# Phase 3 of an encoder layer: the norms listed before the merges, nine 12 KB pieces for its large operands, four buffers for the rows of x

## The chip, the cores and the metric

The kernel runs on one core of one Trainium2 chip. The metric is the device time of one execution in microseconds; before the change the median of 3 runs is 3186.42 us (3184.72 to 3188.18). The engines are named as in the profile: PE (TensorE, matrix products), with PEld for its weight loads, DVE (VectorE), ACT (ScalarE), POOL (GpSimd) and SP (SyncE, which here issues every DMA). PE writes to PSUM; ACT and DVE read PSUM, POOL does not.

## The reference

One layer of an encoder with two request groups, a prompt of 512 tokens and a sample of 1024, with a model width of 1024. All is float32. The part that matters here is the end of the layer:

```python
    merged = g[:, :, 0] * (att @ w_proj_attn) + g[:, :, 1] * (y_ssm @ w_proj_ssm)
    return merged @ w_out
...
        x = x + rmsnorm(m, norm_post_mix[l])
        h = rmsnorm(x, norm_pre_ffn[l])
        gate, up = jnp.split(h @ w_gate_up[l], 2, axis=-1)
        f = (jax.nn.silu(gate) * up) @ w_down[l]
        x = x + rmsnorm(f, norm_post_ffn[l])
```

`g` are sigmoid gates, `att` and `y_ssm` the results of differential attention and of a bidirectional state-space scan. `w_gate_up` is 1024 x 5632, that is gate and up of 2816 columns each.

## The kernel before

The 1536 tokens of both groups are worked on together, in three chunks `c` of 512 (chunk 0 is the prompt). Each float32 operand of a large product is split into two fp32r halves: `hi`, a cast, and `lo`, the rest (`split`, L133: with `act_dve` ACT casts in L135 and DVE subtracts in L136; with `act_pool` ACT casts in L141 and POOL subtracts in L142). A product is three matmuls, hi x hi, hi x lo, lo x hi (`gemm`, L164 to L169).

Phase 3 begins at L872. For each chunk it has three steps:

- the merge: `load_merged(0)` for chunk 0, whose two branches were already merged in phase 2, and `merge(c, ...)` for chunks 1 and 2, which multiplies `w_proj_attn` by the attention's rows and adds the other branch. The result is a pair `hi`, `lo` of 8 x 512 columns (`big_pair`);
- `out_proj`: 16 products of 128 tokens by 256 columns with `w_out`, copied into four tiles `mt`, with sums of squares;
- `norms(c, ...)`: on DVE the first norm (L1066), the added rows of x (loaded in halves into `xr`, L1065, added in L1067), squares on ACT into the same `xr` (L1068), the second norm (L1074); then 32 transposes on PE (L1078), copies `hr` to SBUF (L1080) and stores to `h2` in DRAM (L1081, shown as `h_d`).

Then comes the gate-and-up product, in two halves of 768 tokens. Each half is multiplied by a fast scheme with seven products per block instead of eight: for each of the 22 blocks `jb` of 128 columns of gate and of up, `weights` makes seven weight operands (three of them sums made on POOL, L989, L990, L992, L997), and `gate_up` runs seven products of 12 matmuls and puts them together on DVE. The seven activation operands, `b11`, `t2`, `t3`, `t1`, `b21`, `t4`, `b22` in the order of their products, are made once for each half by `Operands` from rows of `h2` (`rw`, L928): `t2`, `t3`, `t1` and `t4` are sums and differences. The first `NPRE` = 2 blocks run with single buffers in the pool `mp` and make silu from tanh, since `norms(2)` uses the same space; from the third block on a pool `fw` takes the place of `mp`.

All pairs and operands are tiles of one pool, `big`: seven slots of 16 KB a partition. A pair takes two slots, an operand (12 KB) one. A tile waits until an earlier user of its slot is done.

The order of instructions in each engine's queue is set while the program is built, by a planner that simulates the program and lets each engine take, of the instructions that are ready in its simulation, the one listed first. On the chip each queue runs strictly in that order. The places are thus the order of listing in L1087 to L1107 for the norms, merges and operands, and each engine's queue for what then stands behind what. The listing that the change touches:

```python
            t0 = out_proj(m0)
            m1 = merge(1, aT1)
            norms(0, t0)
            aT2 = att(2)
            t1 = out_proj(m1)
            m2 = merge(2, aT2)
            norms(1, t1)
            ops = Operands(0, wk, "araw", 3)
            ops.build_first()
            ops.build(("b21",), V, "act_dve")
            t2 = out_proj(m2)
            ops.build(("t4",), V, "act_dve")
```

Of the kernel before, what the change touches and what calls it, by code (L numbers as in the profile page):

```python
# [10 lines left out]
F32 = mybir.dt.float32  # L11
I32 = mybir.dt.int32
F32R = mybir.dt.float32r
AF = mybir.ActivationFunctionType
ALU = mybir.AluOpType
# [3 lines left out]
P = 128  # L19
D = 1024  # L20
KB = D // P
# [9 lines left out]
SEGK = 120  # L31
SKP = 2304
PU = (1, 1)
OT = ("gt", 2)
NG = 2
YE = ("act_pool",) * 4
RATIO = 0.5
# [1 line left out]
IA = 1  # L39
AHEAD = (0,)  # L40
XRB = 2
NPRE = 2
CB = (1, 1)
RWB = 7
NW = 0
NKEEP = 1
SEQS = ((0, 4), (4, 12))
GROUPS = ((0, 512), (512, 1024))
# [29 lines left out]
def hybrid_trunk_kernel(ctx: ExitStack, tc: tile.TileContext, a: dict, y_prompt, y_sample):  # L78
    nc = tc.nc
    V, S, G, TE = nc.vector, nc.scalar, nc.gpsimd, nc.tensor  # L80
# [3 lines left out]
    def f(ap):  # L84
        return ap.bitcast(F32)
# [273 lines left out]
    with ExitStack() as ph1:  # L359
# [18 lines left out]
        with tc.tile_pool(name="xa", bufs=2, reuse_waits="tile") as xa, tc.tile_pool(name="xa_ps", bufs=3, space=PSUM) as xps:  # L378
            natural_log_exp()
            later = []  # L380
            for c in range(NCH):
                dst = hp.tile([P, 2, KB, 512], F32R, tag="hT", name=f"hT{c}")
                tiles = []
# [134 lines left out]
        for d_ in range(2):  # L518
            for o in (0, 1024):
# [6 lines left out]
                     tag="wraw")  # L526
# [343 lines left out]


    with ExitStack() as ph3:  # L872
        big = ph3.enter_context(tc.tile_pool(name="big", bufs=7, reuse_waits="tile"))
        wk = ph3.enter_context(tc.tile_pool(name="wk", bufs=2, reuse_waits="tile"))
        wy = ph3.enter_context(tc.tile_pool(name="wy", bufs=1, reuse_waits="tile"))
        mm = ph3.enter_context(tc.tile_pool(name="mm", bufs=6, space=PSUM, reuse_waits="tile"))
# [3 lines left out]
        def mm_tile(n):  # L880
            return mm.tile([P, n], F32, tag="mm", name="mm")

        def big_pair():
            return [big.tile([P, KB, 512], F32R, tag="big", name="big") for _ in range(2)]

        def load_merged(c):
            hi, lo = big_pair()
            for k in range(0, KB, 2):
                both = mp.tile([P, 2, 512], F32, tag="mt", name="both", bufs=4)
                load(out=both, in_=part_d[k * P:(k + 2) * P, c * 512:(c + 1) * 512].rearrange("(a p) t -> p a t", p=P))  # L890
                S.activation(out=hi[:, k:k + 2], in_=both, func=AF.Copy, scale=0.5)
                V.scalar_tensor_tensor(lo[:, k:k + 2], both, 0.5, f(hi[:, k:k + 2]), op0=ALU.mult, op1=ALU.subtract)
            return hi, lo

        def merge(c, aTt):
# [21 lines left out]
        class Operands:  # L917
# [4 lines left out]
            def __init__(self, t0, pool, tag, bufs):  # L922
                self.t0, self.pool, self.tag, self.bufs, self.tiles = t0, pool, tag, bufs, {}
# [4 lines left out]
                load(out=x, in_=h2_d[r0:r0 + P, n0:n0 + 384])  # L928
                return x

            def build_first(self):
                b11, t2, t3, t1 = [big.tile([P, 2, 4, 384], F32R, tag="big", name="op") for _ in range(4)]
                self.tiles.update(b11=b11, t2=t2, t3=t3, t1=t1)
                for k in range(4):
                    x, y, z = self.raw(0, 0, k), self.raw(0, 1, k), self.raw(1, 1, k)
                    split(b11[:, 0, k], b11[:, 1, k], x[:], "act_dve")
                    V.tensor_sub(z, z, y)
                    split(t3[:, 0, k], t3[:, 1, k], z[:], "act_dve")
                    V.tensor_sub(y, y, x)
                    split(t1[:, 0, k], t1[:, 1, k], y[:], "act_dve")  # L940
                    V.tensor_add(x, x, z)
                    split(t2[:, 0, k], t2[:, 1, k], x[:], "act_dve")

            def build(self, names, add, eng):
                for name in names:
# [89 lines left out]
        with ExitStack() as ph3a:  # L1035
# [17 lines left out]
            def norms(c, arg):  # L1053
                tiles, sums = arg
                v, r, t_ = [wk.tile([P, 2, 4], F32, tag=n, name=n) for n in ("mv", "mr", "mt_")]
                s2 = wk.tile([P, 4, 2], F32, tag="ms2", name="ms2")
                V.reduce_sum(v[:, 0], sums, axis=mybir.AxisListType.X)
                V.tensor_scalar(v[:, 0], v[:, 0], 1.0 / D, EPS, op0=ALU.mult, op1=ALU.add)
                rsqrt(r[:, 0], v[:, 0], t_[:, 0])
                for j, mt in enumerate(tiles):  # L1060
                    t = 4 * c + j
                    for o in (0, 512):
                        mo = mt[:, o:o + 512]
                        xt = mp.tile([P, 512], F32, tag="xr", name="xr", bufs=2)
                        load(out=xt, in_=rows(t, a["x_prompt"], a["x_sample"])[:, o:o + 512])  # L1065
                        V.scalar_tensor_tensor(mo, mo, r[:, 0, j:j + 1], pmw[:, o:o + 512], op0=ALU.mult, op1=ALU.mult)  # L1066
                        V.tensor_add(mo, mo, xt)  # L1067
                        S.activation(out=xt, in_=mo, func=AF.Square, accum_out=s2[:, j, o // 512:o // 512 + 1])  # L1068
                    store(out=x2_d[t * P:(t + 1) * P, :], in_=mt)
                V.tensor_add(v[:, 1], s2[:, :, 0], s2[:, :, 1])  # L1070
                V.tensor_scalar(v[:, 1], v[:, 1], 1.0 / D, EPS, op0=ALU.mult, op1=ALU.add)
                rsqrt(r[:, 1], v[:, 1], t_[:, 1])
                for j, mt in enumerate(tiles):
                    V.tensor_scalar(mt, mt, r[:, 1, j:j + 1], 0.0, op0=ALU.mult, op1=ALU.add)  # L1074
                for k in range(KB):
                    ps = tr_ps.tile([P, 512], F32, tag="tr", name="tr_ps")
                    for j, xn in enumerate(tiles):
                        TE.transpose(ps[:, j * P:(j + 1) * P], xn[:, k * P:(k + 1) * P], ident)  # L1078
                    hr = (mp if k % 2 else wk).tile([P, 512], F32, tag=("gt", "xr")[k % 2], name="hr", bufs=2)
                    S.activation(out=hr, in_=ps, func=AF.Copy, scale=cols[:, C_FFN + k:C_FFN + k + 1])  # L1080
                    store(out=h2_d[k * P:(k + 1) * P, c * 512:(c + 1) * 512], in_=hr)  # L1081

# [5 lines left out]
            att_scale(1, zq, msq, ap, tr_ps, "tr")  # L1088
            aT1 = att(1)
            t0 = out_proj(m0)  # L1090
            m1 = merge(1, aT1)
            norms(0, t0)
            aT2 = att(2)
            t1 = out_proj(m1)
            m2 = merge(2, aT2)
            norms(1, t1)
            ops = Operands(0, wk, "araw", 3)
            ops.build_first()
            ops.build(("b21",), V, "act_dve")
            t2 = out_proj(m2)  # L1100
            ops.build(("t4",), V, "act_dve")
            ops.tag, ops.bufs = OT
            ops.build(("b22",), V, "act_pool")
            w = {jb: weights(jb, "pt", 1) for jb in range(NPRE + NW)}
            for jb in range(NPRE):
                gate_up(0, jb, ops.all(), w[jb], mp, 1, False)
            norms(2, t2)  # L1107

        with tc.tile_pool(name="fw", bufs=2, reuse_waits="tile") as fw:
            for jb in range(NPRE, FB):  # L1110
                if jb >= NPRE + NW:
                    w[jb] = weights(jb, rpool=fw if jb > NPRE else None)
                gate_up(0, jb, ops.all(), w[jb], fw, 2)
            ops = Operands(768, fw, "rw", RWB)
            ops.build_first()
            ops.build(ops.names[4:], G, "act_dve")
            for jb in reversed(range(FB)):
                if jb < FB - NKEEP:
                    w[jb] = weights(jb, rpool=fw)
                gate_up(768, jb, ops.all(), w[jb], fw, 2)  # L1120
# [104 lines left out]
```

## Time and profile before

| | |
|---|---|
| median of 3 runs | 3186.42 us |
| the profiled execution | 3193.28 us |
| its span, first to last instruction | 3191.5 us |
| PE busy | 3035.2 us (95%) |
| DVE busy | 1826.8 us (57%) |
| ACT busy | 1260.0 us (39%) |
| POOL busy | 650.7 us (20%) |
| mean granted clock of PE | 0.980 |

The profile is of one execution. In its groups a line is followed by the engine, the operation, the output and input tiles by name, the shapes, the count, the busy time and the mean of one in ns, then the idle time of the engine just before and what ended it. `L167 <- ACT whi L135: 18.5, 2, 15.6` in the view of waits reads: instructions of line 167 waited for ACT's line 135 writing `whi`, 18.5 us in all, 2 times, 15.6 us the longest. A timeline gives the start, the duration, the instruction, and in brackets the idle time before it and its releaser. Matmuls are pipelined, so that a matmul's own duration is longer than the distance to the next.

### The profile page before, as it was taken

The page shows a single profiled execution, that of the slowest core. Times are in us where ns is not written, and L with a number is a line of the kernel's source. Part 1 is how long each engine was busy: PE and PEld are TensorE (multiplying, and loading weights), DVE is VectorE, ACT ScalarE, POOL GpSimd, SP SyncE. Part 2 cuts the span into 40 slices and gives each one's busy share as a digit, 9 for nine tenths or more (in the row PEclk, how much of TensorE's full clock was granted, in tenths as well). Part 3 has the DMA queues.
Part 4 walks back from the last instruction along what each step waited for, and adds up shares of the span by engine and source line. Part 5 has one row for each costly group of instructions (what it writes and reads, how often), then busy time and mean ns, then how long its engine had stood idle before and what let it go on. Part 6 is the DMA issues. An engine that isn't in the chain of part 4 may idle for free. (4 is left out here: it accounts for less than half of the span.)

```text
span 3191.5 us, 44134 instructions
## 1 busy us (share of the span) xinstructions
PE 3035.2 (95%) x16667; PEld 2672.3 (84%) x16667; DVE 1826.8 (57%) x2957; ACT 1260.0 (39%) x2305; POOL 650.7 (20%) x508
## 2 busy tenths in 40 slices
PE   7999999999999999899999898978999999989998
PEld 7988887888787777788877787878999899978887
DVE  5214444455327996387778845676666766632444
ACT  4103333333303333366666645543333333332443
POOL 0001111000133442243232100023333433300000
PEclk9999999999999999999999999989999999999999
DMA  4633333223554445755546047644333333363454
GB/s 149 195 99 112 110 105 108 59 77 106 156 166 139 146 143 150 213 174 165 168 135 186 27 139 240 214 145 130 98 103 101 100 98 100 108 202 97 125 163 132
DMA packets 441341, 429.44 MB, mean 135 GB/s; under 512 B 25200, under 2 KB 358481, under 8 KB 440017
## 3 DMA queue, kind: packets, MB, share of 16 engines
q1 hardware_dynamic: 441129, 426.63, 43.2%
q8 instruction: 131, 2.15, 0.3%
q14 instruction: 81, 0.66, 0.1%
HBM read 314.48 MB, written 120.44 MB: 136 GB/s over the span
## 5 line engine op out<-in xcount | busy, mean ns | idle before, releaser
L167 PE MATMUL acc<-hT,whi 128*128 128x512 f32 x1056 | 421.6, 399 | 3.4 <-ACT st L453 3.4
L168 PE MATMUL acc<-hT,whi 128*128 128x512 f32 x1056 | 417.1, 395 | 0.0
L169 PE MATMUL acc<-hT,wlo 128*128 128x512 f32 x672 | 262.5, 391 | 0.0
L167 PEld LDWEIGHTS acc<-hT,whi 128*128 128x128 f32 x1056 | 199.1, 189 | 49.1 <-issue 5.8
L299 ACT ACTIVATE pt<-pt,nm 128x1024 f32<-128x1024 f32 (+1 forms) x192 | 193.1, 1006 | 111.3 <-DVE nm L296 108.0
L168 PEld LDWEIGHTS acc<-hT,whi 128*128 128x128 f32 x1056 | 199.2, 189 | 42.6 <-issue 3.6
L296 DVE CUSTOM_DVE_ANT_0 pt<-s,tb 128x1024 f32<-128x1024 f32 (+1 forms) x192 | 197.5, 1040 | 53.0 <-PE s L294 41.0
L167 PE MATMUL acc<-whi,hT 128*128 128x256 f32 x768 | 224.9, 293 | 1.2 <-ACT hT L206 0.6
L169 PE MATMUL acc<-whi,hT 128*128 128x256 f32 x768 | 225.1, 294 | 0.4 <-DVE hT L207 0.3
L168 PE MATMUL acc<-wlo,hT 128*128 128x256 f32 x768 | 223.3, 291 | 0.0
L167 PE MATMUL d<-dhi,fh 128*128 128x512 f32 x528 | 207.1, 392 | 5.9 <-ACT fh L135 5.9
L169 PE MATMUL d<-dhi,fl 128*128 128x512 f32 x528 | 206.8, 392 | 4.2 <-DVE fl L136 4.2
L168 PE MATMUL d<-dlo,fh 128*128 128x512 f32 x528 | 206.8, 392 | 0.0
L135 ACT CAST whi<-wraw 128x1024 fp32r<-128x1024 f32 (+1 forms) x115 | 115.9, 1036 | 214.0 <-PE acc L169 82.9
L136 DVE TENSOR_TENSOR fl<-raw,fh 128x896 fp32r<-128x896 f32 (+1 forms) x70 | 79.5, 1137 | 193.7 <-ACT fh L135 193.7
L167 PE MATMUL mm<-op,wy 128*128 128x384 f32 x528 | 178.9, 339 | 8.6 <-ACT op L135 6.9
L234 POOL TENSOR_TENSOR ql<-raw,qh 128x512 fp32r<-128x512 f32 x48 | 64.7, 1362 | 575.0 <-ACT qh L231 575.0
L169 PE MATMUL mm<-op,wy 128*128 128x384 f32 x528 | 178.7, 339 | 0.0
L168 PE MATMUL mm<-op,wy 128*128 128x384 f32 x528 | 178.4, 338 | 0.0
L136 DVE TENSOR_TENSOR wlo<-wraw,whi 128x1024 fp32r<-128x1024 f32 x80 | 95.4, 1221 | 112.9 <-ACT whi L135 103.5
L167 PEld LDWEIGHTS acc<-whi,hT 128*128 128x128 f32 x768 | 147.9, 193 | 11.7 <-issue 9.6
L169 PE MATMUL acc<-hT,whi 128*128 128x512 f32 x384 | 156.3, 407 | 0.0
(356 smaller groups left out, 8200.5 us busy)
## 6 DMA issues: line engine op xcount, KB each, us to landing
wraw<-in_w_in_dram SPq DMA_DIRECT2D x60, 512.0 KB
wraw<-in_w_gate_up_dram SPq DMA_DIRECT2D x92, 256.0 KB
raw<-ff_d SPq DMA_DIRECT2D x46, 448.0 KB
wr<-in_w_gate_up_dram SPq DMA_DIRECT2D x80, 256.0 KB
ff_d<-c SPq DMA_DIRECT2D x88, 192.0 KB
g_d<-st SPq DMA_DIRECT2D x48, 256.0 KB
xg<-xs_d SPq DMA_DIRECT2D x48, 256.0 KB
gt<-g_d SPq DMA_DIRECT2D x48, 256.0 KB
```

The costliest lines, as they stand in the source:

```text
L135: S.copy(hi, raw)
L136: V.tensor_sub(lo, raw, f(hi))
L167: TE.matmul(ps, ah, bh, start=(i == 0), stop=False)
L168: TE.matmul(ps, ah, bl, start=False, stop=False)
L169: TE.matmul(ps, al, bh, start=False, stop=(i == n - 1))
L234: G.tensor_sub(q_l[:, s_], q_r[:, s_], f(q_h[:, s_]))
L296: V.tensor_tensor_reduce(out=pt[:], in0=sps[:], in1=tb[:, off:off + SL], scale=-1.0, scalar=3.0e38, op0=ALU.add, op1=ALU.min, accum_out=nm ...
L299: S.activation(out=pt, in_=pt, func=AF.Exp, bias=nm[:, m:m + 1], scale=-1.0, accum_out=(z0, zs[:, 0:1])[m])
```

## The change

The pool `big` has nine slots of 12 KB instead of seven of 16 KB (108 KB instead of 112). A pair is now three slots: each holds three of the eight blocks of 512 columns, both their `hi` and `lo`; a small class `Part` maps the index `k` to the slot. An operand still takes one slot. `load_merged` converts each loaded pair of blocks in two steps of 512 columns instead of one of 1024.

`norms(0)` and `norms(1)` are listed ahead of `merge(1)` and `merge(2)`. The rows `xr` have four buffers instead of two; every second `hr` uses them, and the first half's operands take their rows from them instead of from `araw` (three buffers) and, for `b22`, `gt` (two). `t4` is listed ahead of `out_proj(2)`; the weights of block 0 are listed ahead of `b22`, whose subtraction goes from POOL to DVE; the weights of the other early blocks are listed one block at a time. `NPRE` is 4 instead of 2.

For the second half `build_first`, which loads three rows for each k-block and makes four operands of them, gives way to `build` by terms: `b11` and `t2` with their sums on POOL, `t3` and `t1` with theirs on DVE, each loading its own rows (1, 3, 2 and 2 for each k-block instead of 3 together). Its `b21`, `t4` and `b22` are as before.

```diff
-OT = ("gt", 2)
...
-NPRE = 2
+NPRE = 4
...
-        big = ph3.enter_context(tc.tile_pool(name="big", bufs=7, reuse_waits="tile"))
+        big = ph3.enter_context(tc.tile_pool(name="big", bufs=9, reuse_waits="tile"))
...
+        class Part:
+
+            def __init__(self, tiles, part):
+                self.tiles, self.part = tiles, part
+
+            def __getitem__(self, at_):
+                k = at_[1]
+                return self.tiles[k // 3][(at_[0], self.part, k % 3) + at_[2:]]
+
         def big_pair():
-            return [big.tile([P, KB, 512], F32R, tag="big", name="big") for _ in range(2)]
+            tiles = [big.tile([P, 2, 3, 512], F32R, tag="big", name="big") for _ in range(3)]
+            return Part(tiles, 0), Part(tiles, 1)
...
-                S.activation(out=hi[:, k:k + 2], in_=both, func=AF.Copy, scale=0.5)
-                V.scalar_tensor_tensor(lo[:, k:k + 2], both, 0.5, f(hi[:, k:k + 2]), op0=ALU.mult, op1=ALU.subtract)
+                for i in range(2):
+                    S.activation(out=hi[:, k + i], in_=both[:, i], func=AF.Copy, scale=0.5)
+                    V.scalar_tensor_tensor(lo[:, k + i], both[:, i], 0.5, f(hi[:, k + i]), op0=ALU.mult, op1=ALU.subtract)
...
-                        xt = mp.tile([P, 512], F32, tag="xr", name="xr", bufs=2)
+                        xt = mp.tile([P, 512], F32, tag="xr", name="xr", bufs=4)
...
-                    hr = (mp if k % 2 else wk).tile([P, 512], F32, tag=("gt", "xr")[k % 2], name="hr", bufs=2)
+                    hr = (mp if k % 2 else wk).tile([P, 512], F32, tag=("gt", "xr")[k % 2], name="hr", bufs=(2, 4)[k % 2])
...
             t0 = out_proj(m0)
+            norms(0, t0)
             m1 = merge(1, aT1)
-            norms(0, t0)
             aT2 = att(2)
             t1 = out_proj(m1)
+            norms(1, t1)
             m2 = merge(2, aT2)
-            norms(1, t1)
-            ops = Operands(0, wk, "araw", 3)
+            ops = Operands(0, mp, "xr", 4)
             ops.build_first()
-            ops.build(("b21",), V, "act_dve")
+            ops.build(("b21", "t4"), V, "act_dve")
             t2 = out_proj(m2)
-            ops.build(("t4",), V, "act_dve")
-            ops.tag, ops.bufs = OT
-            ops.build(("b22",), V, "act_pool")
-            w = {jb: weights(jb, "pt", 1) for jb in range(NPRE + NW)}
+            w = {0: weights(0, "pt", 1)}
+            ops.build(("b22",), V, "act_dve")
             for jb in range(NPRE):
+                if jb:
+                    w[jb] = weights(jb, "pt", 1)
                 gate_up(0, jb, ops.all(), w[jb], mp, 1, False)
             norms(2, t2)
...
             ops = Operands(768, fw, "rw", RWB)
-            ops.build_first()
+            ops.build(ops.names[:2], G, "act_dve")
+            ops.build(ops.names[2:4], V, "act_dve")
             ops.build(ops.names[4:], G, "act_dve")
```

More of the change, by code (lines that the diff above doesn't have):

```diff
@@ L41 @@
 XRB = 2
-NPRE = 2
+NPRE = 4
 CB = (1, 1)
 RWB = 7
-NW = 0
 NKEEP = 1
@@ L929, in raw, with build_first @@
                 return x
-            def build_first(self):
-                b11, t2, t3, t1 = [big.tile([P, 2, 4, 384], F32R, tag="big", name="op") for _ in range(4)]
-                self.tiles.update(b11=b11, t2=t2, t3=t3, t1=t1)
+            def build_first(self, names=("b11", "t2", "t3", "t1")):
+                o = {n: big.tile([P, 2, 4, 384], F32R, tag="big", name="op") for n in names}
+                self.tiles.update(o)
                 for k in range(4):
                     x, y, z = self.raw(0, 0, k), self.raw(0, 1, k), self.raw(1, 1, k)
[L936 to L942, printed above, removed]
+                    for n, t_, m, s_ in (("b11", x, None, None), ("t3", z, z, y), ("t1", y, y, x), ("t2", x, x, z)):
+                        if m is not None and (n in o or n != "t1"):
+                            (V.tensor_add if n == "t2" else V.tensor_sub)(t_, m, s_)
+                        if n in o:
+                            split(o[n][:, 0, k], o[n][:, 1, k], t_[:], "act_dve")
             def build(self, names, add, eng):
@@ L1110, in hybrid_trunk_kernel @@
             for jb in range(NPRE, FB):
-                if jb >= NPRE + NW:
-                    w[jb] = weights(jb, rpool=fw if jb > NPRE else None)
+                w[jb] = weights(jb, rpool=fw if jb > NPRE else None)
                 gate_up(0, jb, ops.all(), w[jb], fw, 2)
             ops = Operands(768, fw, "rw", RWB)
-            ops.build_first()
+            ops.build(ops.names[:2], G, "act_dve")
+            ops.build(ops.names[2:4], V, "act_dve")
             ops.build(ops.names[4:], G, "act_dve")
```

## The prediction

> **What bounds the kernel now.** I read the page first, for the engine that is full:
>
> ```profile
> span 3191.5 us, 44134 instructions
> PE 3035.2 (95%) x16667; PEld 2672.3 (84%) x16667; DVE 1826.8 (57%) x2957; ACT 1260.0 (39%) x2305; POOL 650.7 (20%) x508
> ```
>
> PE is the bound, so only time in which PE stands or runs slowly can be won. The change touches phase 3 alone, about 1840 to 2800 us. So I cut that phase into stages in the table of windows (columns: stretch, its length, busy time and instructions of PE, PEld, DVE, ACT, POOL, granted clock, DMA share, GB/s):
>
> ```profile
> 2100.00:2185.00 85.00, 53.19 (x275) 48.33 (x274) 63.04 (x110) 32.94 (x71) 30.59 (x19) 0.82 0.49 156
> 2470.00:2500.00 30.00, 19.42 (x81) 18.56 (x81) 29.85 (x44) 14.06 (x30) 18.73 (x13) 0.77 0.37 110
> 1895.00:1960.00 65.00, 59.88 (x305) 50.64 (x306) 53.55 (x96) 32.69 (x63) 0.00 (x0) 0.97 0.82 277
> 1960.00:1985.00 25.00, 19.65 (x143) 19.02 (x142) 6.31 (x8) 15.49 (x39) 0.00 (x0) 0.86 0.49 162
> 2060.00:2100.00 40.00, 39.10 (x327) 38.80 (x326) 21.46 (x36) 25.91 (x72) 0.00 (x0) 1.00 0.55 183
> 2650.00:2700.00 50.00, 50.00 (x289) 50.00 (x288) 31.27 (x56) 17.05 (x34) 16.67 (x14) 1.00 0.35 106
> ```
>
> The last row is the gate-and-up product undisturbed: 50 / 289 = 0.173 us a matmul, and 84 matmuls (seven products of 12) make 14.5 us for a block `jb`. Against it three places are poor: the entry to the first half of that product (2100 to 2185), the change of halves (2470 to 2500), and the seam after the first merge (1960 to 1985). In the view of waits, PE in 2100 to 2185:
>
> ```profile
> PE mm L167 <- ACT whi L135: 18.5, 2, 15.6
> PE tr_ps L1078 <- DVE mt L1074: 7.7, 1, 7.7
> PE mm L169 <- DVE whi L136: 2.1, 1, 2.1
> PE mm L167 <- ACT c L1021: 1.7, 1, 1.7
> PE tr_ps L1078 <- ACT hr L1080: 0.9, 2, 0.6
> PE mm L169 <- DVE wlo L136: 0.8, 1, 0.8
> ```
>
> Together 31.7 us. After the 15.6 us the clock is low as well; PE's timeline there:
>
> ```profile
> 2117.96 0.69 PE L167 MATMUL mm<-op,whi 128*128 128x384 f32 x1 [15.57 <-ACT whi L135]
> ...
> 2124.73 0.52 PE L168 MATMUL mm<-op,wlo 128*128 128x384 f32 x1
> 2125.05 0.38 PE L167 MATMUL mm<-op,wlo 128*128 128x384 f32 x1
> ```
>
> From 2118 to 2125 a matmul follows the last after 0.32 us; 7 us at about half speed lose some 3.4. So about 35 of the 85 us are lost. Why `whi` is late stands in POOL's timeline:
>
> ```profile
> 2109.42 4.13 POOL L142 TENSOR_TENSOR op<-rw,op 128x384 fp32r<-128x384 f32 x2 [301.13 <-DVE rw L951]
> 2113.51 1.66 POOL L989 TENSOR_TENSOR s<-wraw 128x512 f32<-128x512 f32 x1
> 2115.24 2.01 POOL L990 TENSOR_TENSOR s<-s,wraw 128x512 f32<-128x512 f32 x1
> ```
>
> PE's second product needs `s2` (L990) of the first block's weights. That stands on POOL behind `b22`'s subtractions (L142), which wait for a slot that `out_proj(2)` frees. DVE is just then building `t4`, which waits for a slot too.
>
> **Entry to the first half: -25 us.** Seven slots less `m2`'s two left five for operands until `out_proj(2)` ended: `b11`, `t2`, `t3`, `t1`, `b21`. Nine slots less three leave six, so `t4` (12 adds and 4 splits on DVE) moves under `out_proj(2)`, where DVE is busy 21.46 of 40 us. With `b22` off POOL and listed after `weights(0)`, nothing stands ahead of L989 and L990, which here follow L142 with no wait of their own. So the first wait, the 2.1 behind it and the slow clock go: 15.6 + 2.1 + 3.4 = 21. Next late is `b22`, alone behind `out_proj(2)` now: PE needs it six products later, 6 x 12 x 0.173 = 12.5 us. A row of `h2` takes some 5 us to land (below) and its four pieces are cast and subtracted in some 3 (4 x 0.55 and a cast), so it is in time by 4; if its loads come in two rounds, 1 us late.
>
> The 7.7 us are `norms(2)`: its transposes stood after two blocks, now after four, with 29 us more PE work as cover. That cover is used by DVE. Its prices, from the groups of 1890 to 1965, then of 2100 to 2185:
>
> ```profile
> L1067 DVE TENSOR_TENSOR mt<-mt,xr 128x512 f32<-128x512 f32 x8 | 5.5, 688 | 0.6 <-DMA xr<-in_x_prompt_dram 0.6
> ...
> L1066 DVE SCALAR_TENSOR_TENSOR mt<-mt,mr,pmw 128x512 f32<-128x512 f32 x8 | 5.4, 750 | 0.0
> L1074 DVE TENSOR_SCALAR mt<-mt,mr 128x1024 f32<-128x1024 f32 x4 | 2.8, 749 | 0.0
> L184 DVE TENSOR_TENSOR mt__17030<-mr 128x4 f32<-128x4 f32 x6 | 1.0, 162 | 0.2
> ```
>
> ```profile
> L136 DVE TENSOR_TENSOR wlo<-s,wlo 128x512 fp32r<-128x512 f32 x7 | 5.0, 745 | 2.1 <-ACT wlo L135 2.1
> ...
> L1013 DVE SCALAR_TENSOR_TENSOR c<-th,c 128x384 f32<-128x384 f32 x4 | 2.2, 552 | 0.0
> ```
>
> One `norms`: 5.4 + 5.5 + 2.8 and 26 small steps of 0.16 = 18 us. A block with the tanh form: 11 steps of 0.55 and 7 splits of 0.7 = 11 us; the two blocks more in that form cost 4 steps, 2.2 us of it. Four blocks less the first weights (done under `out_proj(2)`), `norms(2)` and `b22` (2.2): 39 + 18 + 2 = 59 us on DVE, against 4 x 14.5 = 58 of matmuls and 32 transposes on PE. That is even, but for POOL: each block has four POOL steps of about 1.3 us, 21 us for four. What DVE loses beside POOL is seen at the change of halves:
>
> ```profile
> 2487.61 0.54 DVE L1022 TENSOR_TENSOR c<-mm,c 128x384 f32<-128x384 f32 x1
> ...
> 2493.70 7.40 DVE L136 TENSOR_TENSOR op<-rw,op 128x384 fp32r<-128x384 f32 x8
> ```
>
> Eight splits of 0.55 took 7.4, 3.0 more, and POOL is busy 18.73 of those 30 us, so 4.6 of the 7.4: DVE loses 0.65 of POOL's time. A `c` add, which reads PSUM, kept its 0.54. With 7 of 18 steps of that kind I take half of 21, 10 us (bounds 0 and 14). Single `c` buffers and one pair of raw weights, which cost 0.8 + 1.7 now, I take at 2 more. So some 10 of the 35 us stay: **-25**, bounds -35 and -5 (only POOL's queue mended).
>
> The Trainium skill, SBUF — State Buffer, section "Who interferes with whom", has DVE and GpSimd hold their shared ports by an exclusive lock. The trace agrees in part, the splits by 0.65 of POOL's time; by the full lock DVE would lose 21 instead of 10, and this term would be -14.
>
> **Change of halves: -7 us.**
>
> ```profile
> 2473.77 0.69 PE L167 MATMUL mm<-op,whi 128*128 128x384 f32 x1 [3.66 <-ACT op L135]
> 2492.89 1.10 PE L167 MATMUL mm<-op,wy 128*128 128x384 f32 x2 [6.92 <-ACT op L135]
> ```
>
> 81 x 0.173 = 14 of 30 us, so 16 are lost: 10.6 in these waits, the rest by the clock of 0.77. Two spare slots now let `b11` and `t2` be built during the blocks before, where DVE has 19 of 50 us free, so the first wait goes. But PE then comes about 5 us earlier to `t4`, whose adds on POOL begin only after `b21`:
>
> ```profile
> 2480.07 5.66 POOL L951 TENSOR_TENSOR rw<-op 128x384 f32<-128x384 f32 x3 [11.09 <-DVE op L136]
> ```
>
> So the gain is what `t4` gains. DVE had 28 steps ahead of `b21`'s (16 splits, 12 adds), and has 16 (`t3`, `t1`): 12 x 0.55 = 6.6. I take -7, bounds -16 and 0. Building by terms costs 20 loads more:
>
> ```profile
> L928 SPq DMA_DIRECT2D rw<-h_d x40: 319/320/743, 1962.5 to 2495.1; - x40
> ```
>
> 20 x 0.32 = 6.4 us of SP's queue and 3.9 MB, where the DMA share is 0.35: nothing, with PE's blocks as cover; without cover 6.4.
>
> **Norms first: -4 us.** In 1890 to 1985 PE waits
>
> ```profile
> PE mm L169 <- DVE wlo L136: 3.8, 2, 2.2
> PE mm L167 <- ACT msq L1050: 3.8, 1, 3.8
> ```
>
> The second comes from `msq` waiting for a buffer behind stores of `h2` (`hr`), at the end of `norms(0)`, inside `out_proj(1)`. Listed first and with four row buffers, the norms end inside the merge, so it goes; the first, a panel split behind other DVE work, stays. What moves ahead of a merge on SP's queue is 8 loads of x and 12 stores, 20 x 0.32 = 6.4 us of issues; behind them stand the merge's panels, its gates and parts, and the panel in hand (48 matmuls of 512 columns, some 10 us) covers them; without that PE would wait those 6.4. `norms(1)` ends earlier too, so the operands' rows start earlier; they share the four buffers with x and `hr`, so a row can wait for a store on SP with `w_out`'s panels behind it. A round costs a landing, from the chain:
>
> ```profile
> 2073.85 4.85 DMA rw<-h_d
> ```
>
> Four rounds for the first four operands and one for `b21`, 24 us, and the 16 steps of `t4`, 9, fit into the 40 us of `out_proj(2)`. Bounds: -15 (all that seam, with its clock of 0.86) and +45 (third rival).
>
> **Entry of the phase: 0.** `load_merged` works in halves:
>
> ```profile
> L892 DVE SCALAR_TENSOR_TENSOR big<-both,big x4: 1218/1220/1222, 1846.8 to 1850.6; 128x1024 fp32r<-128x1024 f32 x4
> ```
>
> 8 x 0.69 instead of 4 x 1.22 is 0.6 us more, but its first piece is ready 0.5 earlier; bounds -1 and +2. In phase 4, other slots come free in another order; the down weights' casts may shift by 2 us either way.
>
> **Sum**: -25 - 7 - 4 = -36. The profiled execution took 3193.28 us (span 3191.5), 7 over the median of 3186.42; I take the difference from the median: **3150 us**.
>
> **The rivals.** *POOL holds DVE for all of its time* in the four blocks: 21 us instead of 10, 11 less gain, 3161. For it: the eight splits; against it: the adds from PSUM. [...] *DVE stays the bound*: 59 us of work with less than 3 idle, and a planner that fixed each queue's order by its own times; the wait for weights turns into waits for splits and `t4` is no earlier; some 6 us are left, 3181. For it: DVE was busy 63 of 85 us; against it: its half-idle `out_proj(2)`. *Norms starve the merge* (slower): in both merges 18 us of `norms` stand in DVE's queue ahead of a panel's split. With its one panel in hand PE stands from 10 us of unbroken norms on, at most 18 us and 3.4 of slow clock, twice 21.4 = 43. With -4 gone: 3186.4 - 32 + 43 = 3197. For it: 53.55 of 65 us of DVE busy in the first merge; against it: the norms' steps are broken by their loads, and the same work in the same stretch cost PE 3.8 us. *Everything goes*: -35 - 16 - 15 = -66, 3120.
>
> **How the numbers follow.** Forecast 0.54, lock 0.13, DVE bound 0.11, starved merge 0.11, everything 0.11. About 0.2%, 6.4 us, is what a measurement tells from no change. Faster: 0.54 + 0.13 + 0.11 = 0.78; same 0.11; slower 0.11. The range leaves out the starved merge and reaches to the rest: 3120 to 3186.
>
> **What would show it.** Right: in the stage after `out_proj(2)` no wait of PE over 5 us; L990 of the first block before `out_proj(2)` ends; four blocks, then the transposes; at the change of halves one wait of PE, for `t4`, instead of two; the norms' transposes inside the merges. Wrong: waits of PE for `wlo` L136 in the merges over 5 us, or DVE full and PE waiting for `c` and `wy` in the four blocks.

## The result, and the profile after

The changed kernel takes **3205.61 us** (median of 6 runs, 3199.01 to 3214.43) where the kernel before takes 3185.1 (6 runs): ratio **1.0063, 95% interval 1.0047 to 1.0079**. It is slower by 0.6%; the forecast was 3150. The profiled execution took 3214.43 us, 21.15 more than the 3193.28 of the one before. The page after:

```profile
span 3212.7 us, 44180 instructions
PE 3044.9 (95%) x16667; PEld 2674.7 (83%) x16667; DVE 1838.6 (57%) x2965; ACT 1260.5 (39%) x2309; POOL 657.9 (20%) x512
```

The engines carry out nearly the same instructions, PE exactly as many; PE stands still or runs slowly for longer. To see where, I took from both traces the starts of the matmuls and added up, for each stage, by how much the distance to the next one exceeds the distance of that shape in undisturbed stretches (0.173 us for 384 columns). This is PE's lost time, waits and slow clock together. The entry is counted to 4 us past the start of the last transpose of `norms(2)`, here and in all runs below:

```
us lost by PE                                           before  after
seam: end of out_proj(0) to end of out_proj(2)           21.8   51.2
entry: from there to just past the norms(2) transposes   40.0   23.3
behind it, up to 25 us before the change of halves        4.9   17.8
change of halves (65 us)                                 16.6   13.1
sum                                                      83.3  105.4
```

The difference, 22.1 us, accounts for the whole difference of the two executions, 21.15. The seam, 207.0 us long before and 237.2 after, lost 29 us more; the entry gained 17 and lost 13 of them again in the blocks behind it; the change of halves gained 3.5. Line numbers after are those before less 2 for `split` and `gemm` (a matmul waits in L165 to L167), and plus 7 to 9 in the merge and the norms (gate rows L914, their tanh L915, their use L919; the norms' transposes L1085, `hr` L1087, its store L1088).

**The seam.** The view of waits, PE in 1895 to 2100 after (it answers to the lines `wlo` L136 and `msq` L1050 of before):

```profile
PE mm L165 <- DVE gt L919: 21.6, 4, 10.1
PE tr_ps L1085 <- ACT hr L1087: 5.9, 6, 1.6
PE tr_ps L1085 <- DVE mt L1081: 3.8, 1, 3.8
PE mm L165 <- ACT msq L1057: 2.6, 1, 2.6
PE mm L167 <- DVE wlo L134: 1.8, 2, 1.2
```

The first line is new: PE has filled the six PSUM buffers that the kernel gives to such products with those of the merge, and waits for DVE to multiply one by its gate row. The wait for `wlo` is smaller than before. The timeline of the same stretch shows why the gate rows are late:

```profile
1935.82 0.92 SPq L1088 DMA_DIRECT2D h_d<-hr  x2
...
1937.71 3.76 SPq L1088 DMA_DIRECT2D h_d<-hr  x4
...
1944.56 0.41 SPq L1088 DMA_DIRECT2D h_d<-hr  x1
...
1945.49 0.48 SPq L914 DMA_DIRECT2D gt<-g_d  x1
...
1950.27 0.63 ACT L915 ACTIVATE gt<-gt 128x512 f32<-128x512 f32 x1 [6.03 <-DMA gt<-g_d]
1950.93 0.69 DVE L919 SCALAR_TENSOR_TENSOR gt<-gt,mm 128x512 f32<-128x512 f32 x1 [14.48 <-ACT gt L915]
...
1951.68 0.80 PE L165 MATMUL mm<-big,whi 128*128 128x512 f32 x1 [9.10 <-DVE gt L919]
```

The first gate row is loaded behind the eighth store of `norms(0)`'s `hr` (2, 4, 1 at 1943.32, and 1), and in SP's waits of 1895 to 2000 its load waits for such a store to land:

```profile
SPq L914 <- DMA h_d<-hr: 1.8, 1, 1.8
```

DVE stands idle for 14.48 us, then PE goes on 0.75 us after DVE began. In the kernel before the gate rows of both merges came in from 1904.3 us on, after from 1945.5 (columns: shortest, median and longest issue in ns, first and last start):

```profile
L905 SPq DMA_DIRECT2D gt<-g_d x16: 319/336/762, 1904.3 to 2054.0; - x16
```
```profile
L914 SPq DMA_DIRECT2D gt<-g_d x16: 319/320/484, 1945.5 to 2088.3; - x16
```

The clock falls with it (table of windows, after: the third value from the end is the granted clock):

```profile
1930.00:1940.00 10.00, 6.60 (x24) 4.16 (x24) 5.74 (x10) 4.77 (x7) 0.00 (x0) 0.52 0.69 208
1940.00:1950.00 10.00, 1.97 (x8) 1.57 (x8) 0.00 (x0) 2.50 (x4) 0.00 (x0) 0.50 0.96 330
1950.00:1960.00 10.00, 8.32 (x24) 6.59 (x25) 5.47 (x8) 3.73 (x6) 0.00 (x0) 0.61 0.46 134
```

**Entry and behind it.** PE's waits in 2130 to 2265 after; the 15.6 us for `whi` are gone, in their place stand many short ones:

```profile
PE mm L165 <- DVE c L1033: 9.1, 2, 5.8
PE mm L165 <- ACT whi L133: 4.6, 3, 2.9
PE tr_ps L1085 <- DVE c L1020: 2.8, 1, 2.8
```

**Change of halves**, PE in 2455 to 2535 after; before there were 10.6 us for `op`:

```profile
PE mm L165 <- DVE c L1034: 3.2, 1, 3.2
PE mm L166 <- DVE op L134: 3.0, 2, 2.7
PE mm L165 <- DVE c L1033: 1.1, 1, 1.1
```

### The profile page after: what moved, and what is told of

It reads as the page before. It is cut to its first block, busy times and chain, and to the rows that moved or that the text cites. A ratio compares the mean times of both kernels' runs of the same rounds, so it can differ in the third digit from the quotient of the medians.

```text
span 3212.7 us, 44180 instructions
## 1 busy us (share of the span) xinstructions
PE 3044.9 (95%) x16667; PEld 2674.7 (83%) x16667; DVE 1838.6 (57%) x2965; ACT 1260.5 (39%) x2309; POOL 657.9 (20%) x512
## 4 chain that ended last, share of the span: by engine, by line
PE 65%; DMA 12%; DVE 9%; issue 5%; ACT 4%; POOL 3%; SPq 1%; ACTq 0%; DVEq 0%; POOLq 0%
PE acc L165 9%; PE acc L167 9%; PE acc L166 9%; PE mm L165 5%; PE mm L166 4%; PE mm L167 4%; PE d L167 4%; PE d L166 4%; PE d L165 4%; DMA raw<-k_d 1%; DMA araw<-r_d 1%; DMA wraw<-in_w_gate_up_dram 1%; DMA gt<-g_d 1%; PE s L291 1%; PE t L306 1%
## 5 line engine op out<-in xcount | busy, mean ns | idle before, releaser
L165 PE MATMUL acc<-hT,whi 128*128 128x512 f32 x1056 | 421.3, 399 | 3.6 <-ACT st L451 3.6
L167 PE MATMUL acc<-hT,wlo 128*128 128x512 f32 x672 | 262.2, 390 | 0.0
L165 PEld LDWEIGHTS acc<-hT,whi 128*128 128x128 f32 x1056 | 199.1, 189 | 49.8 <-issue 5.8
L165 PE MATMUL acc<-whi,hT 128*128 128x256 f32 x768 | 224.2, 292 | 0.5 <-ACT hT L204 0.4
L167 PE MATMUL acc<-whi,hT 128*128 128x256 f32 x768 | 224.0, 292 | 0.4 <-DVE hT L205 0.3
L165 PE MATMUL d<-dhi,fh 128*128 128x512 f32 x528 | 206.5, 391 | 5.9 <-ACT fh L133 5.9
L167 PE MATMUL d<-dhi,fl 128*128 128x512 f32 x528 | 206.1, 391 | 4.2 <-DVE fl L134 4.2
L165 PE MATMUL mm<-op,wy 128*128 128x384 f32 x528 | 179.5, 340 | 1.5 <-ACT c L1028 1.1
L167 PE MATMUL mm<-op,wy 128*128 128x384 f32 x528 | 179.5, 340 | 0.0
L167 PE MATMUL acc<-hT,whi 128*128 128x512 f32 x384 | 156.3, 407 | 0.0
L165 PEld LDWEIGHTS acc<-whi,hT 128*128 128x128 f32 x768 | 147.5, 192 | 10.5 <-issue 9.2
L133 ACT CAST fh<-raw 128x896 fp32r<-128x896 f32 (+1 forms) x70 | 68.8, 984 | 218.2 <-PE d L166 190.2
```

The source lines that it names most:

```text
L133: S.copy(hi, raw)
L165: TE.matmul(ps, ah, bh, start=(i == 0), stop=False)
L167: TE.matmul(ps, al, bh, start=False, stop=(i == n - 1))
```

## The experiments

**Why are the gate rows late?** Theory A: the rows `gt` of a merge, every second `hr` of the norms and `msq` are tiles of one tag with two buffers, and the tiles of a tag take its buffers in the order of listing. With the norms listed first, the merge's gate rows wait until the norms are over and their `hr` stored. The prediction's own rival was DVE's queue. The first run takes the sharing away, the second the order, the third brings the order alone into the kernel before.

```diff
-                    hr = (mp if k % 2 else wk).tile([P, 512], F32, tag=("gt", "xr")[k % 2], name="hr", bufs=(2, 4)[k % 2])
+                    hr = mp.tile([P, 512], F32, tag="xr", name="hr", bufs=4)
```

> The changed kernel, with all eight rows hr of a norm in the four xr buffers, so that the norms no longer use the two gt buffers that the merge's gate rows use. From the end of the first output projection to the end of the third the changed kernel took 237 us, the kernel before 207. Theory A (shared gt buffers: the tiles of a tag take its buffers in the order of listing, so the merge's gate rows wait until the norms' hr are stored): that stretch falls to 205 to 212 us, the gate rows of the first merge are loaded before 1920 us and no PE wait in a merge is over 3 us; the time is 3175 to 3183. Theory B (18 us of norms stand in DVE's queue ahead of the merge's work): the stretch stays within 5 us of 237 and the time at 3200 to 3210, since DVE's order of listing is untouched. Theory C (the norms' loads and stores stand ahead of the gate rows on SP's queue): most of it stays, 225 to 237 us, time over 3193.

Measured: 3169.82 us, ratio to the kernel before 0.9955 [0.9937, 0.9973]; seam 197.9 us, further down than theory A's 205 to 212, lost 13.1. The gate rows and PE's waits in 1885 to 2090 of that run:

```profile
L914 SPq DMA_DIRECT2D gt<-g_d x16: 319/339/1297, 1895.0 to 2040.8; - x16
```
```profile
PE mm L167 <- DVE wlo L134: 3.2, 2, 2.4
PE mm L165 <- ACT big L921: 2.4, 3, 1.0
```

One line of code makes the slower kernel faster than the one before: the wait for `gt` is gone, with the norms still listed first.

```diff
-            norms(0, t0)
             m1 = merge(1, aT1)
+            norms(0, t0)
...
-            norms(1, t1)
             m2 = merge(2, aT2)
+            norms(1, t1)
```

> The changed kernel with norms(0) and norms(1) listed behind merge(1) and merge(2) again; all else as changed. All three theories give the stretch from the first output projection to the third back, 205 to 212 us, and a time of 3174 to 3182: the rest of the change by itself, 4 to 10 us under the kernel before. If the loss had come from the 12 KB pieces or from four xr buffers, the stretch would stay over 225 us and the time over 3193.

Measured: 3175.48 us, 0.9975 [0.9961, 0.9989]; seam 203.3 us, lost 18.4. The order alone also ends the loss, as A has it.

The kernel before with nothing but the inverse of that edit, the norms first:

> The kernel before with nothing changed but the listing of norms(0) and norms(1) ahead of the merges (two xr buffers, seven slots). Theory A: the gate rows wait as in the changed kernel, and longer, as two xr buffers slow the norms: the stretch grows to 235 to 250 us, the time to 3212 to 3230. Theory B: 18 us of norms in each merge less the panel in hand, 8 to 18 us each: 3200 to 3222. If listing the norms first costs nothing by itself, 3180 to 3190.

Measured: 3220.43 us, 1.0119 [1.01, 1.0137]; seam 250.7 us, lost 64.7, the gate rows from 1943.2 us on. PE's waits in 1895 to 2130 there, with only two buffers for the rows of x:

```profile
PE tr_ps L1078 <- DVE mt L1074: 18.4, 2, 11.5
PE mm L167 <- DVE gt L910: 12.6, 4, 5.3
```

A has the right sign; the larger wait there, for the second norm (L1074), has no run of its own. To tell the end of the sharing from more buffers, a later run gave the even `hr` two buffers of their own and had only two of `xr`, with the operands' rows in `araw` (three) as before; it has the second half's old build too (below), which by itself left the seam at 238.9 us. The lines are set against the version of the first run:

```diff
-                        xt = mp.tile([P, 512], F32, tag="xr", name="xr", bufs=4)
+                        xt = mp.tile([P, 512], F32, tag="xr", name="xr", bufs=2)
...
-                    hr = mp.tile([P, 512], F32, tag="xr", name="hr", bufs=4)
+                    hr = mp.tile([P, 512], F32, tag=("hg", "xr")[k % 2], name="hr", bufs=2)
...
-            ops = Operands(0, mp, "xr", 4)
+            ops = Operands(0, wk, "araw", 3)
```

> The changed kernel with the second half's old build, where every second copy hr has two buffers of its own, the others and the rows of x share two, and the first half's operands take their rows from the three buffers of araw again. So the merge's gate rows share their buffers with no hr, and there are not four row buffers anywhere. Theory A (the merge's gate rows waited for buffers that the norms listed ahead of them held): the seam, from the end of out_proj(0) to the end of out_proj(2), falls from 237 to 198 to 210 us, with the first gate row loaded before 1905 us, and the ratio to the kernel before is 0.993 to 0.998. Rival (the four row buffers made the run with hr in xr fast, not the end of the sharing): the seam stays at 225 us or more and the ratio at 1.002 or more.

Measured: 3174.82 us, 0.9968 [0.9951, 0.9984]; seam 197.9 us, gate rows from 1896.5 us:

```profile
L914 SPq DMA_DIRECT2D gt<-g_d x16: 320/332/455, 1896.5 to 2044.8; - x16
```

Theory A stands and the rival falls. And with the sharing gone, is the order of the listing worth anything? The fastest version (every `hr` in `xr`, old build) with the norms behind the merges:

> The fastest version so far (every hr in the four buffers xr, the second half's old build) with both norms listed behind the merges, as in the kernel before. If the order of the listing is worth something of its own once no gate row waits for an hr, the seam is 3 to 8 us longer than that version's 197 and the time 3 to 10 us above it (ratio to the kernel before 0.995 to 0.997). Rival: only the sharing counted, and the seam and the time are the same within 2 us and 4 us.

Measured: 3170.02 us, 0.9948 [0.9931, 0.9964]; seam 197.6 us, against 3167.74 us and 197.3 of the same version with the norms first, run beside it (below). The rival holds as far as these runs can tell: only the sharing counted. With the norms behind the merges the seam was 203.3 us with the sharing and 197.6 without it (one profile each), so the order of the kernel before seems to pay for it too.

**What is lost again behind norms(2)?** Theory P: the early build of `b11` and `t2`. POOL's timeline after shows it among the sums for the weights (L996 to L1004), 15 to 34 us behind the last transpose of `norms(2)` (2213.3) and some 250 ahead of the change of halves:

```profile
2232.74 2.44 POOL L965 TENSOR_TENSOR rw<-rw 128x384 f32<-128x384 f32 x2
2235.14 1.73 POOL L996 TENSOR_TENSOR s<-wr,wraw 128x512 f32<-128x512 f32 x1
2236.83 1.61 POOL L999 TENSOR_TENSOR s<-wr 128x512 f32<-128x512 f32 x1
2238.41 2.75 POOL L965 TENSOR_TENSOR rw<-rw 128x384 f32<-128x384 f32 x2
```

```diff
-            ops.build(ops.names[:2], G, "act_dve")
-            ops.build(ops.names[2:4], V, "act_dve")
+            ops.build_first()
```

> The changed kernel with the second half's operands made by build_first as before. Theory P (making b11 and t2 early puts eight POOL adds between the weights' POOL steps at 2220 to 2265 us, and this loses about 10 us there, while the change of halves gains 3 to 5): 5 to 10 us less than the changed kernel, 3196 to 3201, with PE losing under 3 us in the 60 us behind the transposes of norms(2). Rival (the early build is free and the losses there come from the end of the single-buffered stage): no gain there, and the change of halves loses 4 us: 3206 to 3212.

Measured: 3201.34 us, 1.0056 [1.0039, 1.0072]; lost behind `norms(2)` 10.0 us instead of 17.8, change of halves 10.2 instead of 13.1. Both edits together:

> Both: all rows hr in the four xr buffers, and the second half's operands made by build_first as before. The first alone gave 0.9955 of the kernel before, the second alone gave 4 us on the changed kernel. Theory P (the early b11 and t2 cost PE in the blocks behind norms(2), 11 us there, and gain 4 at the change of halves): 4 to 8 us under the first alone, 0.993 to 0.9945 of the kernel before, and a loss of PE in the 100 us behind the transposes of norms(2) of some 8 us instead of 12. Rival (that loss is the tail of the single-buffered stage and the 4 us were noise): 0.9945 to 0.996, no difference in those 100 us.

Measured: 3158.84 us, **0.9936 [0.9915, 0.9957]**; once more, measured beside the run with `hr` in buffers of its own:

> The fastest version so far again, beside the three others of this call: every hr in the four buffers xr, and the second half's old build. Ratio to the kernel before 0.9915 to 0.9957 as in its first run; if the difference to the run with hr in xr alone was chance, 0.9955 or more.

Measured: 3167.74 us, 0.9938 [0.9921, 0.9954]. It beats both kernels. What the old build is worth behind `norms(2)` shows in the profiles, 8 us in the changed kernel, but with every `hr` in `xr` only 2.5 to 2.7 (13.5 with the new build, 11.0 and 10.8 with the old); in the times it is inside the intervals (1.0056 against 1.0063, 0.9936 against 0.9955). P asked for a loss under 3 us in the first 60 us; 8.0 stayed there, where the new build lost 10.6, so most of the 8 us lie further on. P also had the new build gain 3 to 5 us at the change of halves, where the old one lost 2.9 less. Nor does the edit take the early start away: ACT casts seven pieces of these operands between 2218 and 2250 us with the old build, eight between 2224 and 2252 with the new. What it moves is the sums, from POOL, among those for the weights, to DVE. So the new build costs something, sums on POOL may be a part of it, and by what path most of it arises isn't shown.

**What holds the entry?** In the fastest version 37 (first profile) and 40.5 us (second) are still lost from `out_proj(2)` to the change of halves, where the kernel before lost 44.9: the gain, 4 to 8 us, is a third of the 25 forecast or less. It is near the 6 us of the rival "DVE stays the bound", which had a chance of 0.11. First, two early blocks instead of four:

> The kernel of e5 with NPRE = 2: two blocks ahead of norms(2) instead of four. Theory N (norms(2)'s DVE steps need the four blocks as cover; with two PE waits for the second norm, as before the change): a wait of PE for L1081 of 5 to 8 us returns, the time is 5 to 12 us over e5. Rival S (the single c buffers and the norm's steps between a block's adds cost about as much for each further block as the cover gains): within 3 us of e5.

Measured: 3164.17 us, 0.9941 [0.9924, 0.9958], lost 42.1. The wait for the second norm that theory N asked for doesn't come back, and the number of early blocks is worth nothing that these runs can tell.

Then the single buffer `c11` (theory S) against DVE's work (theory D); for the room, both of these are the fastest version with three row buffers instead of four:

```diff
-                             for t_, b_ in (("c11", bufs), ("c12", bufs), ("c22", min(bufs, CB[1])))]
+                             for t_, b_ in (("c11", 2), ("c12", bufs), ("c22", min(bufs, CB[1])))]
```

> The kernel of e5 with three xr buffers instead of four: the control for the next run, which needs the space. If the fourth buffer carries the gain between the first and the third output projection, that stretch grows from about 198 us to 203 or more and the time by 4 to 10 us; if any number over two does, both stay within 3 us.

> The kernel of x3 with two c11 buffers in the blocks ahead of norms(2). Theory S (block 1's first copy waits 7 us on ACT for the store of block 0's c11, which stands behind norms(2)'s steps on DVE, and PE then waits 7.8 us for a PSUM tile): those two waits go and the time is 4 to 8 us under x3. Theory D (DVE's amount of work is the bound of that stage, whatever the buffers): the wait moves to c12 or to the weights' splits, and the time stays within 3 us of x3.

Measured: 3169.98 us, 0.9964 [0.995, 0.9978], without, and 3168.59 us, 0.9957 [0.9942, 0.9972], with the second buffer. PE's waits in 2090 to 2215, first with one, then with two:

```profile
PE mm L165 <- ACT c L1028: 7.1, 2, 5.0
PE mm L166 <- DVE op L134: 5.4, 4, 1.8
```
```profile
PE mm L165 <- DVE c L1029: 8.3, 1, 8.3
PE mm L165 <- ACT whi L133: 5.8, 3, 3.4
```

The wait moves from ACT's copy to the next step, DVE's, and S falls for `c11`. The same single buffer of `c12` has no run: in the fastest version's second profile the add into it (L1029) waits 2.3 us for the store of the block before. (Three row buffers instead of four left the seam as it was, 196.6 us, but 45.3 us were lost behind it, against 37 and 40.5.)

Four runs then took work out of `norms(2)` in the fastest version: the eight scalings by the first norm (6 us of DVE), those and the eight adds with their loads of x, the loads alone, and the sixteen steps alone. The first edit:

```diff
+                        if c < 2:
                             V.scalar_tensor_tensor(mo, mo, r[:, 0, j:j + 1], pmw[:, o:o + 512], op0=ALU.mult, op1=ALU.mult)
```

> The fastest version so far, leaving out the eight steps of norms(2) that scale the third chunk's rows by the first norm (6 us of DVE work; the outputs of that chunk are wrong by that factor). Theory D (the entry to the gate-and-up product is bound by DVE's work between out_proj(2) and the end of norms(2)): the loss of PE at the entry, 26 us, falls by 4 to 6 us, and the time with it. Rival (PE waits there for single buffers and for weights, DVE only shows the delay): the loss falls by less than 2 us.

> The fastest version so far, leaving out the scaling by the first norm and the adding of the rows of x for the third chunk in norms(2): sixteen DVE steps, 11 to 12 us, and eight loads. Twice the dose of the run that left out eight. Theory D (DVE's work between out_proj(2) and the end of norms(2) is the bound): the losses of PE at the entry, behind norms(2) and in the rest of the half, 40.5 us together, fall by 8 to 12, and the time with them. Rival (DVE isn't the bound: what is taken from it comes back as waits for weights and single buffers, as the run with eight steps less did, 39.2 against 40.5 us): the sum falls by less than 4 us.

> The fastest version with the old raw pieces, leaving out the eight loads of x for the third chunk in norms(2): the add takes the norm's weights instead of the rows of x, so every DVE step stays. Theory D (it is the time of DVE's steps that binds the entry): the losses of PE from out_proj(2) to the change of halves stay at 37 to 41 us and the ratio at 0.9935 or more. Rival L (it is the loads of x and the steps' waits for them, in four buffers shared with hr and the operands' rows): the losses fall to 33 us or less, the ratio to 0.992 or less.

> The other half of the run without norm and x: the third chunk's scaling by the first norm and its add of x are left out, the eight loads stay and so does the squares' wait for the buffers. Theory D: the losses fall to 28 to 33 us as in the run that left out both, ratio 0.9905 to 0.992. Rival L: they stay at 36 us or more, ratio 0.993 or more.

```
left out                      entry  behind  us        ratio
nothing, two profiles     26.2, 29.7  11.0, 10.8  3158.84, 3167.74  0.9936, 0.9938
8 DVE steps                   25.1    13.3   3167.76   0.9944 [0.9929, 0.9958]
8 loads                       29.1    12.1   3164.76   0.9926 [0.9909, 0.9943]
16 DVE steps                  21.0    13.3   3162.76   0.9914 [0.9893, 0.9935]
16 DVE steps and 8 loads      17.9    11.9   3156.92   0.9913 [0.9894, 0.9932]
```

The loads are worth nothing at the entry, 29.1 against 26.2 and 29.7; sixteen steps, some 12 us, take 5 to 12 us off it, eight steps 1 to 5. Part of it comes back behind the entry: both columns together are 37.2 and 40.5 whole, 38.4 without eight steps, 34.3 and 29.8 without sixteen. D asked for 28 to 33 where 34.3 came, and its rival for 36 or more. So D holds in its direction: DVE's work makes the entry late, by less than a microsecond for each of its own, and how much less these profiles can't say. The wait that goes (PE's waits over the entry and the blocks behind it, the whole version, then without the sixteen steps) is that for DVE's block adds:

```profile
PE mm L165 <- ACT whi L133: 7.7, 4, 3.0
PE mm L165 <- DVE c L1029: 6.0, 1, 6.0
```
```profile
PE mm L165 <- ACT whi L133: 7.3, 4, 2.5
...
PE mm L165 <- DVE c L1029: 0.4, 1, 0.4
```

In the times, the ratios with sixteen steps less lie 0.0022 to 0.0025 below the same version with all of them, inside their intervals.

**The handover behind norms(2)** (theory W). The weights of the second block behind it have one raw piece in `fw`, whose space comes free with the last store of `hr`. SP's timeline of the fastest version, second profile, and POOL's longest wait:

```profile
2179.67 11.33 SPq L1088 DMA_DIRECT2D h_d<-hr  x8
2191.09 1.02 SPq L981 DMA_DIRECT2D wr<-in_w_gate_up_dram  x2
```
```profile
POOL s L996 <- DMA wr<-in_w_gate_up_dram: 19.3, 1, 19.3
```

```diff
-                w[jb] = weights(jb, rpool=fw if jb > NPRE else None)
+                w[jb] = weights(jb, rpool=fw if jb > NPRE + 1 else None)
```

> The fastest version so far, with both raw pieces of the weights of the second block behind norms(2) in the standing pool rp instead of one of them in fw, whose space comes free only with the last store of h2. Theory W (the loss behind norms(2) comes from those loads: they stand on SP behind the eight stores, are issued at 2191 us and POOL waits 19 us for them, while PE has only the rest of one block in hand): the loss of PE in the 100 us behind norms(2) falls from 9.5 to 3 us or less, and the time by 5 to 8 us. Rival (the engines are late there anyway, and the next wait, for hr, c or wy, takes its place): the loss stays over 7 us and the time within 3 us.

> The fastest version with both raw pieces of the second block behind norms(2) in rp, once more, beside the two others. If that edit is worth the 3 us that its profile shows, the ratio to the kernel before is again 0.992 to 0.994 and the losses from out_proj(2) to the change of halves 34 to 37 us; if it was chance, 0.994 or more and 37 to 41 us.

> The changed kernel itself with that one edit: both raw pieces of the weights of the second block behind norms(2) in the standing pool rp. The seam stays at 235 to 239 us. Theory W: of the 17.8 us that PE loses between norms(2) and the change of halves 6 to 9 go, and the ratio to the kernel before is 1.0035 to 1.0045. Rival (the early build of b11 and t2 with its POOL steps holds the blocks there by itself): less than 3 us go, ratio 1.0055 or more.

Measured: in the fastest version 3161.54 us, 0.993 [0.9908, 0.9952], and again 3160.87 us, 0.9916 [0.9899, 0.9932]; the loss in the 100 us behind `norms(2)` fell from 9.5 (9.7 in its other profile) to 6.9 and 6.7. PE no longer waits there for `whi`; its waits in 2170 to 2230 of the first of them are for DVE:

```profile
PE mm L165 <- DVE c L1030: 2.4, 1, 2.4
PE mm L165 <- DVE c L1029: 1.7, 1, 1.7
```

In the changed kernel itself: 3207.66 us, 1.0071 [1.0049, 1.0093]; 12.7 instead of 17.8 lost behind `norms(2)`, seam 236.7 us, and no gain in the time that the runs can tell. So W is worth some 3 us, half of what was expected, and the next wait takes the rest. In the fastest version the edit gives the lowest ratios of the complete kernels, 0.7 to 0.8% under the kernel before, but their intervals meet those of the version without it.

## Why the prediction was wrong, point by point

**Norms first, -4: the step that failed.** It came as +29. I counted what moves ahead of the merge on SP's queue, 20 issues of 0.32 us with the panel in hand as cover, and on DVE's queue in the rival. I did not count the buffers: every second `hr` stands in `gt`, and `msq` "waiting for a buffer behind stores of `h2`" was the very row that I used for the gain. That wait went from 3.8 to 2.6 us, and the same two buffers made the gate rows come 41 us later, at 1945.5 instead of 1904.3. The rival that ended on the other side, 3197 against 3205.61, had the right place and sign and a wrong mechanism: it asked for waits for `wlo` over 5 us, and 1.8 came. The slow clock that it priced at 3.4 for each merge is seen, and for longer: 0.50 to 0.61 for 30 us in the first. Nor is the listing worth the 4 us once the sharing is gone: 197.3 us with the norms first, 197.6 with them last.

**Entry to the first half, -25: mis-sized.** What it said of POOL and of the four blocks came true: L996 and L997 of the first block ran before `out_proj(2)` ended at 2130, and the transposes came behind four blocks. One wait of PE is over the 5 us that I had allowed, 5.8 for `c`.

```profile
2119.30 1.55 POOL L996 TENSOR_TENSOR s<-wraw 128x512 f32<-128x512 f32 x1 [311.23 <-DMA rw<-h_d]
...
2122.39 1.61 POOL L997 TENSOR_TENSOR s<-s,wraw 128x512 f32<-128x512 f32 x1
```

The 15.6 us went, and the entry lost 16.7 less. DVE's work was counted nearly right: 59 us and 10 beside POOL, that is 69, and in the 85 us of that stage it was busy for 69.44.

```profile
2130.00:2215.00 85.00, 70.25 (x380) 66.40 (x378) 69.44 (x133) 35.34 (x76) 26.41 (x16) 0.94 0.46 147
```

What failed is "so some 10 of the 35 us stay". It set DVE's sum against PE's and took only the excess, with 2 us for single buffers, as lost; but 23.3 were lost while DVE still had 15 of 85 us idle. PE waits there for DVE, and DVE for stores out of single buffers `c` and for ACT's casts:

```profile
DVE c L1029 <- DMA ff_d<-c: 3.9, 2, 2.2
DVE wy L134 <- ACT wy L133: 3.1, 3, 1.8
```

And 13 us came back behind `norms(2)`, at a place priced at nothing: by the profiles 8 of them go with the old build of the second half's operands, where the prediction said "during the blocks before, where DVE has 19 of 50 us free" and asked neither which blocks nor about POOL, and some 5 when the weights' loads no longer stand behind the stores. By what path the new build costs its 8 stays open. The two may overlap; no run has both edits in the changed kernel alone.

**Change of halves, -7: half, and not by building by terms.** The stretch lost 3.5 us less. With the old build in the changed kernel it lost 10.2 us instead of 13.1, so building by terms gained nothing there; what else of the change brought the gain, the spare slots or another part, no run separates. The first wait for `op` went, as foreseen. 3.0 us for `op` stay, but PE waits 4.3 for block adds (`c`) that stand on DVE between splits, while POOL makes `t4`'s sums. DVE's timeline and the window of that stretch:

```profile
2499.42 5.20 DVE L134 TENSOR_TENSOR op<-rw,op 128x384 fp32r<-128x384 f32 x4
```
```profile
2500.00:2510.00 10.00, 6.75 (x27) 6.46 (x26) 9.29 (x10) 3.16 (x8) 10.00 (x10) 0.70 0.27 81
```

Four splits of 0.55 took 5.20, 3.0 more, beside a POOL that is busy all of the time: by that count DVE loses 0.58 of POOL's time, near the 0.65 taken. But POOL's own steps are longer there too:

```profile
2499.39 1.01 POOL L959 TENSOR_TENSOR rw<-rw,op 128x384 f32<-128x384 f32 x1
2500.35 1.33 POOL L958 TENSOR_TENSOR rw<-op 128x384 f32<-128x384 f32 x1
2501.64 1.30 POOL L959 TENSOR_TENSOR rw<-rw,op 128x384 f32<-128x384 f32 x1
2502.91 1.30 POOL L958 TENSOR_TENSOR rw<-op 128x384 f32<-128x384 f32 x1
```

The two engines take turns, some 1.3 us for a step of each: the last of these ends at 2504.21, and the fourth split 0.41 us behind it, at 2504.62. From 2100 to 2800 us of this trace, 32 DVE steps of 384 columns with both inputs in SBUF begin while a POOL instruction runs. In 25 the step ends 0.41 to 0.42 us behind that instruction, whatever was left of it; the other 7 (0.55 us each) begin beside two POOL instructions that are themselves stretched, to 1.73 and 4.35 us. The 62 adds that read PSUM and begin beside POOL kept 0.54 to 0.56. So POOL's busy time holds waiting of its own, and DVE's loss as a share of it tests no lock. The exclusive lock of the Trainium skill (SBUF — State Buffer, section "Who interferes with whom") agrees with these numbers, taken instruction by instruction. What doesn't agree is the prediction's price for it, in which DVE loses all of POOL's time: the steps that read PSUM go on.

**Entry of the phase, 0: right.** The last matmul of `out_proj(0)` starts at 1892.41 us instead of 1893.05, 0.6 earlier, inside the bounds of -1 and +2.

## What to carry to other kernels

Before moving a step ahead of another, list for each of its tiles the buffers that it shares with what it is moved past, not only the queues: two kinds of tile in one small set of buffers are chained in the order of listing, whatever the engines could do. Where two engines are near even, expect much more to be lost than the excess of one sum over the other. And where two engines hold each other up, don't read the busy time of either as work.

## What the runs showed that was not expected

Taking 12 us of DVE steps out of a stage that DVE makes late took 5 to 12 us off PE's loss at the entry, but only 3 to 11 with the blocks behind it, and neither 12 nor 6 us of steps show clearly in the time. And two profiles of one kernel, the fastest version, differ by 3.5 us in the loss at the entry (26.2 and 29.7) with the same order on every engine: a theory about 3 us in that stage can't be decided by one profile.
